# A squared-ReLU MLP whose first product takes both parts of the tokens as one 512-column operand

## The chip, the core and the metric

The kernel runs on one NeuronCore of one Trainium2 chip. Its time is the device time of one execution in microseconds (us). The profile is of one more such execution, taken by the hardware profiler, and it gives the span from the first to the last instruction. The engines are named as in the profile: PE is the matrix engine and PEld its weight loads, ACT is ScalarE, DVE is VectorE, POOL is GpSimd, SP issues most of the DMAs.

## The reference

A two-layer decoder trunk on 256 tokens of 1024 features in float32. Layer 0 is stick-breaking attention and an MLP; a K/V projection is shared by three attention branches; layer 1 is the three-branch sparse attention and an MLP; a last RMSNorm ends it. Both MLPs are the part that is changed:

```python
def sqrelu_mlp(x, w1, w2):
    h = jax.nn.relu(x @ w1)
    return (h * h) @ w2

h = h + sqrelu_mlp(rms_norm(h, norm_gain[layer, 1]), mlp_w1[layer], mlp_w2[layer])
```

with w1 of 1024 x 4096 and w2 of 4096 x 1024, for each of two layers.

## The kernel before

Every large product is made from operands that are split in two parts, a high one (rounded to the matrix engine's float32 form) and a low one (the rest). A product of two split operands is three matmuls: high by high, high by low, low by high. The helper `mm3` (L124 to L127) issues these three for one stationary and one moving operand, each with a weight load of its own.

All 256 tokens are held transposed, features on the 128 partitions: `xt_tiles` (L194) allocates a tile for the high parts (`xh`) and one for the low parts (`xl`), each of 8 feature blocks by 256 tokens, 8 KB a partition. `xt_tr` (L174) transposes four feature blocks of the residual stream on PE into two banks, and `xt_evac` (L184) brings them out: ACT writes the high part with the gain (L190), DVE the low part (L191).

The weights come as one stream of pieces of 1 MB in the order of use. `fetch` issues a piece's DMA on SP; `split` (L79) makes half a piece into its high part on ACT (L89) and its low part on DVE (L90); `step` calls it ahead of need, at most two pieces ahead of the one in use, and three buffers each hold raw, high and low pieces.

An MLP (L227) works in 16 chunks of 256 hidden units. `first(c)` (L250) multiplies: for each of 8 feature blocks k and each of two 128-wide halves f, one `mm3` with a block of w1 as the stationary operand and the 256 tokens as the moving one, so 48 matmuls of 256 columns and 48 loads in a chunk. Both halves of the result lie side by side in one bank (`pu`). Then ACT takes the ReLU of the bank (`mr`, L262), DVE multiplies the bank with it (`ms`, L264), ACT writes the high part (`hh`, L268) and DVE the low one (`hl`, L269). `second` (L234) multiplies the result of an earlier chunk with w2: 24 matmuls of 512 columns into four banks (`acc`) that are summed over all chunks. Chunk c's result is used after `first(c + 1)`; the last two chunks are multiplied together at the end of the MLP. In the first chunk the second half of the feature blocks is still to be transposed: `xt_tr(1)` and `xt_evac` stand between the feature blocks 1 and 2, and no `second` follows before `first(1)`.

The banks `pu` come from a pool of four (`bank2`) that the transposes use too. The 8 KB tiles (`big`) come from a pool of six buffers. The order of instructions on each engine is laid out ahead by the framework's planner, from the program's order and its estimated durations: in the trace some instructions stand ahead of others that come earlier in the text.

Of the kernel before, what the change touches and what calls it, by code (L numbers as in the profile page):

```python
# [7 lines left out]
F32 = mybir.dt.float32  # L8
# [3 lines left out]
OP = mybir.AluOpType  # L12
# [24 lines left out]
def hybrid_kernel(ctx, tc, x, eye, gcols, gfin, wqk, wv, wo0, wkv, wqa, wqb, wqc, wo1, w1, w2, cw1, cw2, cpos, gate_b, consts, out):  # L37
# [10 lines left out]
        return a.bitcast(F32)  # L48

    def big(shape, dt, name):  # L50
        return cp.tile(shape, dt, tag="e", name=name, bufs=6)

    def bank(name, dt=F32):
        return ps.tile([P, 512], dt, tag="a", name=name, bufs=4)
# [1 line left out]
    def bank2(name):  # L56
        return ps.tile([P, 512], F32, tag="z", name=name, bufs=4)

    # the weights in the order of their use: loaded ahead, split in two exact parts
    stream = []  # L60

    def feed(src, n):
# [14 lines left out]
                nc.sync.dma_start(raws[-1], src)  # L77

    def split():  # L79
        """the next half of a piece, split"""  # L80
        j, half = divmod(parts[0], 2)
        parts[0] += 1
        n = stream[j][1]
        if half == 0:
            made.append((wp.tile([P, n], F32R, tag="wh", name="wh", bufs=3),
                         wp.tile([P, n], F32R, tag="wl", name="wl", bufs=3)))
        r = slice(half * n // 2, (half + 1) * n // 2)
        h, lo = made[j]
        nc.scalar.copy(h[:, r], raws[j][:, r])  # L89
        nc.vector.tensor_sub(lo[:, r], raws[j][:, r], f32(h[:, r]))  # L90
        if half:
            fetch()
# [36 lines left out]
    def mm(o, a, b, first, last):  # L129
        nc.tensor.matmul(o, a, b, start=first, stop=last, skip_group_check=True)  # L130

    def tok(xt, k, t):
        return xt[0][:, k, t * P:(t + 1) * P], xt[1][:, k, t * P:(t + 1) * P]

# [19 lines left out]
    npow = cst[:, C_PW:C_PW + 1]  # L154

    def var_of(parts_):
        """mean of squares plus eps, per token"""
        ss = sp.tile([P, 2], F32, name="ss")
        for i, src in enumerate(parts_):
            sq = sp.tile([P, D], F32, name="sq", tag="y")  # L160
            tc.keep_in_program_order(
                nc.scalar.activation(sq[:, 0:src.shape[1]], src, AF.Square, accum_out=ss[:, i:i + 1]))
        v = sp.tile([P, 1], F32, name="v", bufs=4)
        if len(parts_) == 2:
            nc.vector.tensor_add(ss[:, 0:1], ss[:, 0:1], ss[:, 1:2])
        nc.vector.tensor_scalar(v, ss[:, 0:1], 1.0 / D, EPS, op0=OP.mult, op1=OP.add)
        return v
# [4 lines left out]
        return r  # L172

    def xt_tr(half):  # L174
        """four feature blocks of the residual stream, transposed; even blocks in one bank, odd ones in the other"""
        pt = [bank2(f"pt{b}").rearrange("p (j q) -> p j q", j=2) for b in range(2)]
        for b in range(2):
            for j in range(2):
                k = 4 * half + 2 * j + b
                for t in range(T):  # L180
                    nc.tensor.transpose(pt[b][:, j, t * P:(t + 1) * P], hres[t][:, k * P:(k + 1) * P], ident)
        return pt

    def xt_evac(pt, half, gi, xt):  # L184
        """times the gain of each feature, split in two"""
        for j in range(2):
            for b in range(2):
                k = 4 * half + 2 * j + b
                g = gc[:, gi * NK + k:gi * NK + k + 1]
                nc.scalar.activation(xt[0][:, k, :], pt[b][:, j, :], AF.Copy, scale=g)  # L190
                nc.vector.scalar_tensor_tensor(xt[1][:, k, :], pt[b][:, j, :], g, f32(xt[0][:, k, :]),  # L191
                                               op0=OP.mult, op1=OP.subtract)

    def xt_tiles(tag):  # L194
        return big([P, NK, T * P], F32R, f"xh{tag}"), big([P, NK, T * P], F32R, f"xl{tag}")

    def o_evac(oT, po, p):
        nc.scalar.copy(oT[0][:, p, :], po[:, 0:T * P])
# [26 lines left out]
                        res(n, t, acc[n][t])  # L225

    def mlp(layer, gi, xt, mid, ap):  # L227
        """xt holds the first half of the blocks already; mid runs inside the last products"""
        wa, wb = i_m[layer]
        acc = [[None, None], [None, None]]  # L230
        held = []
        r2 = []

        def second(items, order, hook=None):  # L234
            for i, (t, n) in enumerate(order):
                if hook is None and i % 2 == 0:
                    step()
                for c, hT, w in items:
                    for f in range(2):
                        if c == 0 and f == 0:  # L240
                            acc[n][t] = bank(f"acc{t}{n}")
                        mm3(acc[n][t], tok(hT, f, t), cut(w, f * D + n * 512, f * D + (n + 1) * 512),
                            c == 0 and f == 0, c == NFC - 1 and f == 1)
                if hook is not None:
                    hook(i, t, n)

        by_n = [(t, n) for n in range(2) for t in range(T)]
        by_t = [(t, n) for t in range(T) for n in range(2)]

        def first(c):  # L250
            w = W(wa[c])
            pu = bank2("pu")
            for k in range(NK):
                if c == 0 and k == 2:
                    xt_evac(xt_tr(1), 1, gi, xt)
                if k % 4 == 0 and (c or k):
                    step()
                for f in range(2):
                    mm3(pu[:, f * 256:(f + 1) * 256], cut(w, k * 256 + f * P, k * 256 + (f + 1) * P),
                        both(xt, k), f == 0 and k == 0, k == NK - 1)  # L260
            r = ap.tile([P, 512], F32, name="mr")
            nc.scalar.activation(r, pu, AF.Relu)  # L262
            s = ap.tile([P, 512], F32, name="ms")
            nc.vector.tensor_mul(s, pu, r)  # L264
            hh = ap.tile([P, 2, T * P], F32R, name="hh", bufs=3)
            hl = ap.tile([P, 2, T * P], F32R, name="hl", bufs=3)
            sv = s.rearrange("p (f q) -> p f q", f=2)
            nc.scalar.copy(hh, sv)  # L268
            nc.vector.tensor_sub(hl, sv, f32(hh))  # L269
            return hh, hl  # L270

        for c in range(NFC):
            hT = first(c)
            if c == 0:
                for t in range(T):
                    r = sp.tile([P, 1], F32, name="r2", bufs=4)
                    nc.vector.reciprocal(r, var_of([hres[t]]))
                    r2.append(r)
            if 0 < c < NFC - 1:
                second([held.pop(0) + (W(wb[c - 1]),)], by_n)  # L280
            held.append((c, hT))

        def hook(i, t, n):
            res(n, t, acc[n][t], r2[t])
            mid(i)

        second([it + (W(wb[it[0]]),) for it in held], by_t if layer else by_n, hook)

    def layer0(ap):
# [1 line left out]
        warm = bank2("warm")  # L291
        for i in range(8):
            mm(warm, zero[:, 0:P], zero, True, True)
# [44 lines left out]
            for n in range(2):  # L338
                nc.scalar.activation(v[:, t, n * 512:(n + 1) * 512], pv[t][n], AF.Copy, scale=rstd[t])

        oT = big([P, NP, T * P], F32R, "oT_h"), big([P, NP, T * P], F32R, "oT_l")

        live = {}

# [74 lines left out]
        return xn  # L419

    def nsa(xk, pt0, ap):
# [1 line left out]
        gbs = ap.tile([P, 48], F32, name="gbs")  # L423
        nc.scalar.dma_start(gbs, gate_b.to_broadcast([P, 48]))
        pos = ap.tile([P, 2, 16], F32, name="pos")
# [7 lines left out]
                nc.scalar.activation(dst, src, AF.Copy, scale=rstd[t])  # L433

        kd0 = big([P, T, 2 * NG, 2, DH], F32, "kd0")
        kd = [[ap.tile([P, NG, 2, DH], F32, name=f"kd{br}{t}") for t in range(T)] for br in range(2)]
        vs = [ap.tile([P, 2, 256], F32, name=f"vs{t}") for t in range(T)]
        pts = [pt0]
        rstd = []
# [27 lines left out]
        sin = cst[:, C_SIN:C_SIN + 32].rearrange("p (t r) -> p t r", t=T)  # L467

        def rope(src, t, n):
            """src[:, h, 0:16] rotated in place; sin holds (-sin, sin), cos (cos, cos)."""  # L470
            a = ap.tile([P, n, 16], F32, name="ropea", tag=f"ropea{n}")
            b = ap.tile([P, n, 16], F32, name="ropeb", tag=f"ropeb{n}")
            c = cos[:, t:t + 1, :].to_broadcast([P, n, 16])
# [4 lines left out]
            nc.gpsimd.tensor_mul(b[:, :, 8:16], src[:, :, 0:8], s1)  # L478
            nc.gpsimd.tensor_add(src[:, :, 0:16], a, b)

        # compressed blocks: windows of the transposed keys and values, plus positions
        M = NG * NC
        blk = [None, None]

# [26 lines left out]
            nc.vector.tensor_sub(bs[:, :, 1, 0:M], bt, f32(bs[:, :, 0, 0:M]))  # L511
            blk[c] = bs

        # keys of the selected and window branches: rotated, transposed, on either half of the partitions, split
        def keys_rope(br):
            for t in range(T):
                rope(kd[br][t].rearrange("p g a d -> p (g a) d"), t, 2 * NG)
# [31 lines left out]
        gather(1)  # L549
        keys_rope(1)  # L550

        # compressed keys and values
        kT = [big([P, NG, 2, T * P], F32R, f"kT{i}") for i in range(2)]
        ph = bank("ph")
        cw_proj(0, 0)
        keys_tr(0)
# [14 lines left out]
        nc.scalar.activation(hu, hu, AF.Exp, scale=-1.0)  # L571
        nc.vector.tensor_mul(hu, hu, hx)

# [1 line left out]
        gates = ap.tile([P, T, 48], F32, name="gates")  # L575

        def q_proj(n, mid=None):
# [86 lines left out]
                nc.vector.tensor_tensor(vcb[:, g], pvc[0:M, g * DH:(g + 1) * DH][:, None, :].to_broadcast([M, 4, DH]),  # L664
                                        cst[0:M, C_BLK:C_BLK + 4][:, :, None].to_broadcast([M, 4, DH]), op=OP.mult)

        # compressed branch: probabilities times gates, transposed, for heads 8 * hf .. 8 * hf + 7
        def cmp_probs(hf):
            for t in range(T):
                pc = bank("psc")  # L670
# [30 lines left out]
        nc.gpsimd.tensor_copy(w2d, cw2s[:, 0, :, None, :].to_broadcast([P, 2, 2, DH]))  # L701
        vcb = ap.tile([M, NG, 4, DH], F32, name="vcb")
        pcT = ap.tile([M, NG, T * P], F32, name="pcT")
        # selected and window branches, and the gated sum of all three
        cb = cam_b[:, None, :].to_broadcast([P, 2, P])

        def scores(h):
# [92 lines left out]
        turn(0)  # L800
        cmp_tr(0)
        q_rot(r[2], 10, 6)
        oT = big([P, NP, T * P], F32R, "oT_h"), big([P, NP, T * P], F32R, "oT_l")
        scores(3)
        scale(2)
        turn(1)
# [82 lines left out]
def _layout(inp):  # L889
# [4 lines left out]
        return np.ascontiguousarray(v)  # L894

    def blocks(w, nk, cw):
        """[K, N] -> [N / cw, K / (nk * 128), 128, nk * cw]"""
        k, n = w.shape
        return cont(w.reshape(k // (nk * P), nk, P, n // cw, cw).transpose(3, 0, 2, 1, 4)
                    .reshape(n // cw, k // (nk * P), P, nk * cw))  # L900
# [46 lines left out]
```

## Time and profile before

| | |
|---|---|
| time, median of 3 runs | 657.2 us (655.12 to 657.46) |
| span of the profiled execution | 654.1 us |
| PE busy | 640.1 us (98%), 4096 matmuls |
| PEld busy | 563.6 us (86%), 4096 loads |
| DVE busy | 397.3 us (61%) |
| ACT busy | 352.2 us (54%) |
| POOL busy | 57.9 us (9%) |
| DMA | 106.87 MB, mean 163 GB/s |

The profile has no time of the profiled execution other than its span; the three runs lie 1.0 to 3.3 us above that span, which is what lies around the first and the last instruction and the spread from run to run. A busy PE is one with a matmul in its pipe: matmuls overlap, so busy time does not add up to the time that they take from the engine. That is read from the starts of successive matmuls instead.

### The profile page before, as it was taken

To read this page: it belongs to the slowest core of one execution; us is meant where nothing else is said; L and a number is where in the kernel's file an instruction comes from. 1 tells how busy PE (TensorE), PEld (TensorE's weight loads), DVE (VectorE), ACT (ScalarE), POOL (GpSimd) and SP (SyncE) were. 2 spreads that over 40 slices of the span, in tenths; PEclk is the share of its full clock that TensorE was granted. 3 is DMA by queue.
4 is the path that set the end of the run, shared out by engine and by line. 5 is a ranking of instruction groups with operands and counts; after the bars stand their busy time and mean duration, and the time that the engine had idled before them with its cause. 6 is when DMAs were issued, how large, how long until landed. Compare 5 with 4: busy or idle time off the path is not lost.

```text
span 654.1 us, 10023 instructions
## 1 busy us (share of the span) xinstructions
PE 640.1 (98%) x4096; PEld 563.6 (86%) x4096; DVE 397.3 (61%) x558; ACT 352.2 (54%) x588; POOL 57.9 (9%) x91
## 2 busy tenths in 40 slices
PE   8999999999999999999999999999999999999995
PEld 5899887899999998988888987767998989999994
DVE  5665554675454545555899888773765555454544
ACT  5776676364444444444866767662464454444433
POOL 1000000000000000000133334550000000000000
PEclk9999999999999999999999999999999999999999
DMA  8853332545555554555545750101555555555501
GB/s 325 299 181 126 128 97 98 174 147 193 194 193 194 178 196 164 198 171 187 202 156 177 264 191 2 66 1 63 178 195 180 194 189 193 192 193 193 178 18 64
DMA packets 16894, 106.87 MB, mean 163 GB/s; under 512 B 2256, under 2 KB 2512, under 8 KB 4944
## 3 DMA queue, kind: packets, MB, share of 16 engines
q1 hardware_dynamic: 15696, 104.92, 45.5%
q10 hardware_dynamic: 1152, 1.31, 0.7%
q8 instruction: 32, 0.52, 0.3%
q14 instruction: 14, 0.11, 0.0%
HBM read 105.17 MB, written 1.05 MB: 162 GB/s over the span
## 4 chain that ended last, share of the span: by engine, by line
PE 87%; ACT 4%; DVE 4%; DMA 2%; POOL 2%; issue 1%; SPq 0%; POOLq 0%; ACTq 0%; DVEq 0%
PE acc L125 11%; PE acc L126 11%; PE acc L127 11%; PE pu L126 9%; PE pu L127 9%; PE pu L125 9%; PE po L130 4%; PE qk L125 2%; PE qk L126 2%; ACT wh L89 2%; PE qk L127 2%; PE z L130 2%; PE pk L127 2%; PE pk L126 2%; PE pk L125 2%
## 5 line engine op out<-in xcount | busy, mean ns | idle before, releaser
L90 DVE TENSOR_TENSOR wl<-raw,wh 128x1024 fp32r<-128x1024 f32 (+3 forms) x202 | 237.6, 1200 | 181.5 <-ACT wh L89 181.1
L89 ACT CAST wh<-raw 128x1024 fp32r<-128x1024 f32 (+3 forms) x202 | 200.3, 1023 | 213.1 <-issue 103.8
L126 PE MATMUL pu<-xln,wh 128*128 128x256 f32 x512 | 145.0, 283 | 0.0
L127 PE MATMUL pu<-xhn,wl 128*128 128x256 f32 x512 | 144.9, 283 | 0.0
L125 PE MATMUL pu<-xhn,wh 128*128 128x256 f32 x512 | 144.5, 283 | 0.0
L125 PE MATMUL acc<-wh,hh 128*128 128x512 f32 x256 | 100.0, 392 | 0.0
L126 PE MATMUL acc<-wl,hh 128*128 128x512 f32 x256 | 99.7, 391 | 0.0
L126 PEld LDWEIGHTS pu<-xln,wh 128*128 128x128 f32 x512 | 98.1, 192 | 1.4 <-DVE xln L191 0.2
L127 PE MATMUL acc<-wh,hl 128*128 128x512 f32 x256 | 99.2, 389 | 0.0
L125 PEld LDWEIGHTS pu<-xhn,wh 128*128 128x128 f32 x512 | 98.0, 192 | 1.2
L127 PEld LDWEIGHTS pu<-xhn,wl 128*128 128x128 f32 x512 | 98.1, 192 | 0.0
L127 PEld LDWEIGHTS acc<-wh,hl 128*128 128x128 f32 x256 | 48.1, 188 | 10.5 <-DVE hl L269 0.2
L125 PEld LDWEIGHTS acc<-wh,hh 128*128 128x128 f32 x256 | 48.2, 188 | 9.6 <-ACT hh L268 0.5
L126 PEld LDWEIGHTS acc<-wl,hh 128*128 128x128 f32 x256 | 48.2, 188 | 8.8
L125 PE MATMUL qk<-xha,wh 128*128 128x256 f32 x128 | 36.8, 288 | 0.0
L127 PE MATMUL qk<-xha,wl 128*128 128x256 f32 x128 | 36.3, 283 | 0.0
L126 PE MATMUL qk<-xla,wh 128*128 128x256 f32 x128 | 36.2, 283 | 0.0
L739 POOL TENSOR_TENSOR pe<-pe,rs 128x256 f32<-128x256 f32 (+1 forms) x32 | 26.2, 841 | 25.5 <-DVE rs L735 19.8
L268 ACT CAST hh<-ms 128x512 fp32r<-128x512 f32 x32 | 19.9, 622 | 14.6 <-DVE ms L264 14.6
L699 POOL MEMSET kcb<- 128x120 f32 x1 | 0.2, 200 | 291.1 <-PE acc L127 291.1
L125 PE MATMUL acc<-wh,oT_h 128*128 128x512 f32 x64 | 25.6, 400 | 0.0
L125 PEld LDWEIGHTS qk<-xha,wh 128*128 128x128 f32 x128 | 24.5, 191 | 1.1 <-issue 1.0
(188 smaller groups left out, 972.3 us busy)
## 6 DMA issues: line engine op xcount, KB each, us to landing
raw<-in_w SPq DMA_DIRECT2D x64, 1024.0 KB, 4.8
raw<-in_wqk SPq DMA_DIRECT2D x8, 1024.0 KB, 4.9
raw<-in_wo SPq DMA_DIRECT2D x8, 1024.0 KB, 4.8
raw<-in_wkv SPq DMA_DIRECT2D x6, 1024.0 KB, 5.0
raw<-in_cw SPq DMA_DIRECT2D x4, 1024.0 KB, 5.1
raw<-in_wv SPq DMA_DIRECT2D x3, 1024.0 KB, 7.1
raw<-in_wqb SPq DMA_DIRECT2D x2, 768.0 KB, 4.2
raw<-in_wqc SPq DMA_DIRECT2D x2, 768.0 KB, 5.2
```

The lines of the kernel that those rows point to most:

```text
L89: nc.scalar.copy(h[:, r], raws[j][:, r])
L90: nc.vector.tensor_sub(lo[:, r], raws[j][:, r], f32(h[:, r]))
L125: nc.tensor.matmul(o, a[0], b[0], start=first, stop=False, skip_group_check=True)
L126: nc.tensor.matmul(o, a[0], b[1], start=False, stop=False, skip_group_check=True)
L127: nc.tensor.matmul(o, a[1], b[0], start=False, stop=last, skip_group_check=True)
L130: nc.tensor.matmul(o, a, b, start=first, stop=last, skip_group_check=True)
L268: nc.scalar.copy(hh, sv)
L699: nc.gpsimd.memset(kcb, 0.0)
L739: nc.gpsimd.tensor_tensor(s, s, rs[:, t, :][:, :, None].to_broadcast([P, 2, n]), op=OP.mult)
```

## The change

In the first product the high and the low part of the tokens become one moving operand of 512 columns. One wide matmul with the high weights makes both products at once: high by high in columns 0 to 255 of a bank, high by low in columns 256 to 511. A second matmul with the low weights and the high tokens adds its 256 columns to the first half of the bank. Each half f of the chunk now fills a bank of its own, and (but in the first four feature blocks of the first chunk) the banks are filled one after the other. So a chunk has 16 matmuls of 512 and 16 of 256 columns, and 32 loads. The two halves of a bank are then added: ACT copies the upper half to SBUF, DVE adds it to the lower one, and DVE makes max(u, 0) times u in one instruction for the chunk. `hh` and `hl` are made as before.

For the wide operand to be contiguous, the two parts of the tokens lie interleaved by feature block in one tile of 16 KB. There are two such tiles (`x`), which the split attention outputs (`oT`) and keys (`kT`) use too; the pool of 8 KB tiles has three buffers instead of six, and takes the keys `kd` as one tile.

```diff
     def big(shape, dt, name):
-        return cp.tile(shape, dt, tag="e", name=name, bufs=6)
+        return cp.tile(shape, dt, tag="e", name=name, bufs=3)
+
+    def pair(shape, name):
+        return cp.tile([P, 2, *shape], F32R, tag="x", name=name, bufs=2)
...
+    def wide(o, a, xt, k, first, last):
+        mm(o, a[0], xt[2][:, k, :, :], first, False)
+        mm(o[:, 0:T * P], a[1], xt[0][:, k, :], False, last)
...
     def xt_tiles(tag):
-        return big([P, NK, T * P], F32R, f"xh{tag}"), big([P, NK, T * P], F32R, f"xl{tag}")
+        xp = cp.tile([P, NK, 2, T * P], F32R, tag="x", name=f"x{tag}", bufs=2)
+        return xp[:, :, 0, :], xp[:, :, 1, :], xp
...
         def first(c):
             w = W(wa[c])
-            pu = bank2("pu")
-            for k in range(NK):
-                if c == 0 and k == 2:
+            pu = [bank2(f"pu{f}") for f in range(2)]
+            r = ap.tile([P, 512], F32, name="mr")
+            u = ap.tile([P, 512], F32, name="mu")
+            s = ap.tile([P, 512], F32, name="ms")
+
+            ks = [(f, k) for k in range(NK // 2) for f in range(2)] + [(f, k) for f in range(2) for k in range(NK // 2, NK)]
+            for i, (f, k) in enumerate(ks if c == 0 else [(f, k) for f in range(2) for k in range(NK)]):
+                if c == 0 and i == 4:
                     xt_evac(xt_tr(1), 1, gi, xt)
-                if k % 4 == 0 and (c or k):
+                if i % 8 == 0 and (c or i):
                     step()
-                for f in range(2):
-                    mm3(pu[:, f * 256:(f + 1) * 256], cut(w, k * 256 + f * P, k * 256 + (f + 1) * P),
-                        both(xt, k), f == 0 and k == 0, k == NK - 1)
-            r = ap.tile([P, 512], F32, name="mr")
-            nc.scalar.activation(r, pu, AF.Relu)
-            s = ap.tile([P, 512], F32, name="ms")
-            nc.vector.tensor_mul(s, pu, r)
+                wide(pu[f], cut(w, k * 256 + f * P, k * 256 + (f + 1) * P), xt, k, k == 0, k == NK - 1)
+                if k == NK - 1:
+                    q = slice(f * 256, (f + 1) * 256)
+                    nc.scalar.copy(r[:, q], pu[f][:, 256:512])
+                    nc.vector.tensor_add(u[:, q], pu[f][:, 0:256], r[:, q])
+            nc.vector.scalar_tensor_tensor(s, u, 0.0, u, op0=OP.max, op1=OP.mult)
...
-        oT = big([P, NP, T * P], F32R, "oT_h"), big([P, NP, T * P], F32R, "oT_l")
+        oT = pair([NP, T * P], "oT")
+        oT = oT[:, 0], oT[:, 1]
...
-        kd = [[ap.tile([P, NG, 2, DH], F32, name=f"kd{br}{t}") for t in range(T)] for br in range(2)]
+        kdt = big([P, 2, T, NG * 2 * DH], F32, "kd")
+        kd = [[kdt[:, br, t, :].rearrange("p (g a d) -> p g a d", g=NG, a=2) for t in range(T)] for br in range(2)]
...
-        kT = [big([P, NG, 2, T * P], F32R, f"kT{i}") for i in range(2)]
+        kT = pair([NG, 2, T * P], "kT")
+        kT = kT[:, 0], kT[:, 1]
```

## Rows read from the trace of the kernel before

**Rows 1.** The page's first part: busy time, share, number of instructions.

```profile
PE 640.1 (98%) x4096; PEld 563.6 (86%) x4096; DVE 397.3 (61%) x558; ACT 352.2 (54%) x588; POOL 57.9 (9%) x91
```

**Rows 2.** The chain that ended last, by engine.

```profile
PE 87%; ACT 4%; DVE 4%; DMA 2%; POOL 2%; issue 1%; SPq 0%; POOLq 0%; ACTq 0%; DVEq 0%
```

**Rows 3.** Windows, one chunk of layer 0: length, busy times, granted clock, DMA share, GB/s.

```profile
181.90:193.12 11.22, 11.22 (x74) 10.26 (x72) 5.92 (x6) 5.10 (x6) 0.00 (x0) 1.00 0.54 188
```

**Rows 4.** Timeline of PE through that chunk: start us, length us, instruction.

```profile
181.90 0.28 PE L125 MATMUL pu<-xhn,wh 128*128 128x256 f32 x1
182.01 0.28 PE L126 MATMUL pu<-xln,wh 128*128 128x256 f32 x1
...
187.65 0.40 PE L125 MATMUL acc<-wh,hh 128*128 128x512 f32 x1
187.88 0.40 PE L126 MATMUL acc<-wl,hh 128*128 128x512 f32 x1
...
189.04 0.39 PE L125 MATMUL acc<-wh,hh 128*128 128x512 f32 x1
...
192.89 0.39 PE L127 MATMUL acc<-wh,hl 128*128 128x512 f32 x1
193.12 0.28 PE L125 MATMUL pu<-xhn,wh 128*128 128x256 f32 x1
```

**Rows 5.** Timeline of PE, first and last of 16 matmuls of 384 columns.

```profile
371.14 0.33 PE L127 MATMUL pq<-wh,xlq 128*128 128x384 f32 x1
...
373.74 0.34 PE L127 MATMUL pq<-wh,xlq 128*128 128x384 f32 x1
```

**Rows 6.** Groups by line and shape, the weight loads: busy us, mean ns, idle before.

```profile
L126 PEld LDWEIGHTS pu<-xln,wh 128*128 128x128 f32 x512 | 98.1, 192 | 1.4 <-DVE xln L191 0.2
```

**Rows 7.** Groups by line and shape, ACT and DVE.

```profile
L198 ACT CAST oT_h<-po 128x256 fp32r<-128x256 f32 x16 | 6.0, 375 | 9.8 <-PE po L130 9.8
L199 DVE TENSOR_TENSOR oT_l<-po,oT_h 128x256 fp32r<-128x256 f32 x16 | 6.7, 421 | 11.7 <-ACT oT_h L198 11.7
L206 DVE SCALAR_TENSOR_TENSOR hres<-acc,r,hres 128x512 f32<-128x512 f32 x8 | 6.0, 748 | 4.6 <-PE acc L127 4.6
```

**Rows 8.** Timeline of DVE and ACT in that chunk.

```profile
183.22 2.36 DVE L90 TENSOR_TENSOR wl<-raw,wh 128x1024 fp32r<-128x1024 f32 x2 [2.03 <-ACT wh L89]
...
191.73 0.68 DVE L269 TENSOR_TENSOR hl<-ms,hh 128x512 fp32r<-128x512 f32 x1
```

**Rows 9.** Timeline of the first chunk of layer 0, then of layer 1.

```profile
132.36 0.36 PE L125 MATMUL pu<-xhn,wh 128*128 128x256 f32 x1
...
133.74 0.87 DVE L191 SCALAR_TENSOR_TENSOR xln<-pt,gc,xhn 128x256 fp32r<-128x256 f32 x2
...
134.27 0.39 PE L126 MATMUL pu<-xln,wh 128*128 128x256 f32 x1
...
134.76 0.88 DVE L191 SCALAR_TENSOR_TENSOR xln<-pt,gc,xhn 128x256 fp32r<-128x256 f32 x2
...
469.57 0.36 PE L127 MATMUL pu<-xhn,wl 128*128 128x256 f32 x1
...
470.03 0.88 DVE L191 SCALAR_TENSOR_TENSOR xln<-pt,gc,xhn 128x256 fp32r<-128x256 f32 x2 [0.73 <-ACT xhn L190]
470.83 1.22 DVE L90 TENSOR_TENSOR wl<-raw,wh 128x1024 fp32r<-128x1024 f32 x1
471.96 0.87 DVE L191 SCALAR_TENSOR_TENSOR xln<-pt,gc,xhn 128x256 fp32r<-128x256 f32 x2
```

**Rows 10.** Timeline of the last chunk of layer 1.

```profile
636.47 0.60 ACT L262 ACTIVATE mr<-pu 128x512 f32<-128x512 f32 x1 [3.71 <-PE pu L127]
...
637.10 0.69 DVE L264 TENSOR_TENSOR ms<-pu,mr 128x512 f32<-128x512 f32 x1 [2.90 <-ACT mr L262]
...
637.83 0.62 ACT L268 CAST hh<-ms 128x512 fp32r<-128x512 f32 x1 [0.76 <-DVE ms L264]
...
638.34 0.66 PE L125 MATMUL acc<-wh,hh 128*128 128x512 f32 x2
```

More of the change, by code (lines that the diff above doesn't have):

```diff
@@ L802, in nsa @@
         q_rot(r[2], 10, 6)
-        oT = big([P, NP, T * P], F32R, "oT_h"), big([P, NP, T * P], F32R, "oT_l")
+        oT = pair([NP, T * P], "oT")
+        oT = oT[:, 0], oT[:, 1]
         scores(3)
```

## The prediction

> **What bounds the kernel now.** First the busy table: PE has 98% of the span, DVE 61%, ACT 54% [rows 1]. As PE's busy time hides gaps between overlapping matmuls, the chain of waits is next: 87% of it is PE itself, no other engine has over 4% [rows 2]. So the span is mostly the sum of what matmuls take from PE one after the other. For the stretch that is changed I read a window over one chunk: 11.22 us, PE and PE alone busy all through, the granted clock at 1.00 (the 2.4 GHz level), DVE busy 5.92 and ACT 5.10 us, DMA at 0.54 [rows 3]. There are 32 such chunks, some 359 of 654 us. What a matmul really costs is the distance between starts in PE's timeline, not its 0.28 or 0.40 us of length. From 181.90 to 187.65 there are 48 matmuls of 256 columns: 5.75 us, 0.120 each. From 187.65 to 193.12 there are 24 of 512 columns: 5.47 us; the last 17 steps of them, 189.04 to 192.89, are 0.2265 each [rows 4]. And 15 steps of 384 columns, 371.14 to 373.74, are 0.173 each [rows 5]. The three lie on one line: 128 more columns cost 0.053 us, and a matmul of no columns would still cost 0.013 us. So each matmul (with its weight load) has a fixed part of 13 ns, 11% of a 256-column one. That fixed part is what the change can save: the number of columns stays the same, 12,288 a chunk.
>
> **The matmuls.** A chunk loses 48 matmuls of 256 columns and gets 16 of 512 and 16 of 256. One pair costs 0.2265 + 0.120 = 0.3465 us, 16 pairs 5.54 instead of 5.75: 0.21 a chunk, over 32 chunks -6.6 us. All of it lies on the path, as PE is the chain.
>
> No row shows 512 and 256 alternating. At the change from 512 to 256 the first short step is 0.11, and at the change back the first long one 0.23 [rows 4]: together 0.34, so a pair of neighbours costs about its sum, which is the value I take. From the other side: after a change the long ones need some steps to settle, 187.65 to 189.04 being six in 1.39 us, 0.232 each. If the pairs never settle they cost 0.352, a chunk 5.63, and the gain is 0.12 x 32 = 3.8 us. If on the other hand the second product no longer needs to settle, 6 x 0.005 = 0.03 a chunk comes on top, -7.5 us. The sum 0.3465 is nearest to the measured change-over.
>
> The Trainium skill, "TensorE: Matmul & The Clock Gate", section "Back-to-back issue gap", speaks against this gain: it gives the gap at full clock as the columns at 2.4 GHz and about 2.5 ns on top. By that, 512 matmuls fewer would be an estimated 1.3 us, a fifth. The rows at 256, 384 and 512 columns have 13 ns instead, and the sum goes by them.
>
> **The evacuation, in the steady chunks.** Before: one ReLU of 512 columns on ACT, one product on DVE. After: two copies of 256 columns on ACT and two sums on DVE; their nearest rows, of the same shape out of a bank, are 0.375 and 0.421 [rows 7]. Then one combined instruction of 512 columns on DVE, between 0.685 (the low part's subtraction, 0.68 in rows 8) and 0.748 [rows 7]. ACT gets 2 x 0.375 for 0.60: +0.15 a chunk; DVE gets 0.84 + 0.7 for 0.69: +0.85. DVE is then busy 6.8 of 11.0 us, ACT 5.3. I cost this at nothing. Its cover: the low part of a chunk is ready at 192.41 (191.73 + 0.68), while the matmuls that read it follow the next chunk's first product, about 198.9 (193.12 + 5.75): 6.4 us to spare. The split weights that wait behind on the same queues are done at 185.58 [rows 8] and used from 193.12: 7.5 us. An added 1 us uses up neither. If the cover were gone, each microsecond of lateness would cost 32 us.
>
> The banks: a chunk now takes two of the four, filled in turn, the first one free for reading 8 pairs (2.8 us) before the chunk ends. A bank is wanted again two chunks later, after 11 us, but in the first chunk: there the transposes hold two, and the next chunk follows at once. They are given back by the last low part of the tokens, before the first chunk's end; I cost it at nothing, and at a wait of one copy and one sum (0.8) in each layer as its upper end.
>
> **The first chunk of each layer.** A wide matmul reads the low tokens too, so it waits for DVE where the high by high product needed ACT alone; and the last four feature blocks are now used up by the first half f alone, at 0.35 a block instead of 0.72. Layer 0: PE goes on at 132.36 and has four pairs before block 4, so it is there about 133.83. The low parts of blocks 4 and 5 take 133.74 to 134.61, of 6 and 7 134.76 to 135.64 [rows 9]. Block 4 waits 0.35, 5 0.1, 6 0.25, 7 0.1: 0.8, of which PE already waits some 0.25 now (the matmul at 134.27 is 0.15 behind the count, the next 0.1): +0.5. Layer 1: PE goes on at 469.57 with two pairs and a third to do, so it is at block 4 about 470.46. Blocks 4 and 5 are ready at 470.47 and 470.91; then a half weight of 1.22 stands before blocks 6 and 7, which come at 472.40 and 472.83 [rows 9]. In strict order PE would wait about 1.2; if the planner puts the other half's blocks 4 and 5 ahead, 0.5. Now it waits 0.15. I take +0.5 for this layer too: +1.0 in all, with ends at 0.2 (the planner fills every wait) and 1.6.
>
> **The last chunk of each layer.** There the evacuation has only the 24 matmuls of the chunk before for cover. Now ReLU, product and high part take 636.47 to 638.45, and the first matmul that needs them comes behind 638.34 with about 0.1 of wait [rows 10]. After: copy 0.375, sum 0.421, combined 0.72, high part 0.62: 2.14 instead of 1.91, and one hand-over more: +0.3. The first bank's copy and sum are done earlier and don't count. PE waits at these points already, so it is late by most of that: +0.2 a layer, +0.4; ends -0.2 and 1.0.
>
> **The storage.** The 16 KB tiles and the three 8 KB buffers are each taken again only after PE work that comes earlier in PE's own order: the outputs' pair follows the last query projection, the keys' pair the last K/V projection, the second compressed block the transposes that it is computed from. The keys' slices in one tile are disjoint. No DMA is moved or added, and SP's queue waits for the same splits. Nothing new is late: 0, with one DVE instruction (0.5) to either side.
>
> **The sum.** -6.6 + 1.0 + 0.4 = -5.2 on a span of 654.1: 648.9. The runs' median is 3.1 above the span; that part, launch and spread, is unchanged. 657.2 - 5.2 = 652.0.
>
> **Rivals.**
>
> *The pairs don't settle, and the edges cost their upper ends.* -3.8 + 1.6 + 1.0 = -1.2: 656.0, no change that can be told. For it: every row of 512 columns right after a change is 5 to 9 ns over the settled ones. Against it: the step after is shorter by as much (0.11 for 0.12). Chance 0.13.
>
> *The change doesn't do what it says:* the fixed part goes with each 256 columns, the wide operand being run as two pieces. Then the matmuls cost what they cost now and the edges' 1.4 is lost: 658.6, no change. Against it stand three widths on one line [rows 4, 5], the widest with one fixed part. Chance 0.07. By the page named above ("TensorE: Matmul & The Clock Gate" of the Trainium skill, the same section) the estimate is 657.2 - 1.3 + 1.4 = 657.3, close to this case.
>
> *More than counted.* The second product settles at once and the planner fills the first and last chunks: -7.5 + 0.2 - 0.2 = -7.5: 649.7. For it: the planner already orders PE's matmuls around these waits. Chance 0.14.
>
> *The other side: a load that the short matmul does not cover.* Each load takes 192 ns [rows 6], and the short matmul ahead of a wide one occupies PE for 120. If loads did not overlap each other, the wide matmul would wait 72 ns more: 512 x 0.072 = 37 us against a gain of 6.6: about 689, slower. It decides from 10 ns a pair on (5.2 / 512), and from 17 ns ((5.2 + 3.3) / 512) the kernel is slower by more than 3.3 us. Against it: in the stream of 256 columns every load has just such a matmul ahead of it, and the steps are still 0.120. So two loads overlap now. Chance 0.05.
>
> **How the numbers follow.** 0.5% of the time is 3.3 us, about what a measurement of this kernel can tell from no change: faster is below 653.9, slower above 660.5. My forecast, 652.0, has 0.61. Its own unknowns reach from -7.5 to about -3, so nearly all of it is faster (0.58), the rest the same. With the case of a larger gain faster has 0.72; the unsettled pairs and the split operand give the same with 0.03 + 0.13 + 0.07 = 0.23; slower 0.05. The range reaches from 649.4 (the larger gain, and a median that falls lower in its spread) to 656.0 (the unsettled pairs with the edges' upper ends). It leaves out the other two cases and the tails.
>
> **What would show it.** Right: in PE's timeline of a steady chunk, steps of 0.227 and 0.120 in turn, a first product of 5.55 us and a chunk of 11.0. No PE wait for `hh`, `hl` or split weights between the second and the last chunk. In the first chunks PE waits of half a microsecond on the low tokens (L191), in the last ones of a few tenths on the high part. Wrong: a pair at 0.352 or more, which takes 3 us of the gain; at 0.36, which takes all; or a PE wait that comes back in every chunk.

## The result, and the profile after

The changed kernel takes 652.0 us (median of 4 runs, 651.2 to 652.6), the kernel before 657.1 in the same comparison (655.1 to 657.5). The ratio is 0.9933, with a 95% interval from 0.9915 to 0.9952: 4.4 us less, between 3.1 and 5.6 (the two medians themselves lie 5.1 apart). Its profiled execution has a span of 650.8 us and a time of 652.6; 1.8 us lie around the span.

The page after, with the busy table and the chain by engine, for [rows 1] and [rows 2]:

```profile
PE 636.9 (98%) x3584; PEld 536.9 (82%) x3584; DVE 420.4 (65%) x622; ACT 356.7 (55%) x620; POOL 57.0 (9%) x91
...
PE 84%; DVE 6%; ACT 4%; POOL 2%; issue 2%; DMA 1%; POOLq 0%; SPq 0%; ACTq 0%; DVEq 0%
```

There are 512 matmuls and loads fewer, and PE is still the chain. To see where the time went, the span is cut at the starts of the stages. Windows of the kernel before: the start, layer 0's attention, its MLP, K/V and queries, layer 1's attention, its MLP, the tail. The columns are length, busy time of PE, PEld, DVE, ACT and POOL, granted clock, DMA share, GB/s.

```profile
0.00:31.31 31.31, 29.28 (x124) 21.99 (x125) 19.21 (x27) 20.39 (x30) 4.58 (x10) 1.00 0.85 307
31.31:130.13 98.82, 98.12 (x697) 85.77 (x696) 56.53 (x71) 61.51 (x94) 0.00 (x0) 1.00 0.39 136
130.13:311.90 181.77, 181.77 (x1169) 165.86 (x1168) 99.71 (x112) 86.16 (x108) 0.00 (x0) 1.00 0.52 183
311.90:386.59 74.69, 73.16 (x440) 66.16 (x439) 65.34 (x97) 49.99 (x78) 22.50 (x39) 1.00 0.58 203
386.59:466.75 80.16, 77.13 (x510) 59.06 (x510) 55.46 (x138) 48.50 (x171) 29.71 (x40) 1.00 0.18 59
466.75:647.05 180.30, 180.30 (x1160) 164.75 (x1159) 98.91 (x113) 84.21 (x107) 0.55 (x1) 1.00 0.47 167
647.05:654.13 7.08, 0.39 (x2) 0.00 (x0) 2.09 (x4) 1.45 (x3) 0.55 (x1) 0.85 0.21 80
```

The same stages of the changed kernel:

```profile
0.00:32.31 32.31, 29.56 (x125) 22.57 (x125) 18.70 (x27) 20.24 (x30) 2.88 (x10) 0.95 0.80 302
32.31:131.16 98.85, 98.15 (x697) 85.79 (x696) 56.51 (x71) 61.51 (x94) 0.00 (x0) 1.00 0.37 136
131.16:311.25 180.09, 179.79 (x913) 151.88 (x912) 110.86 (x141) 87.52 (x122) 0.00 (x0) 1.00 0.50 184
311.25:385.83 74.58, 73.15 (x440) 66.11 (x439) 66.14 (x99) 50.65 (x81) 22.52 (x39) 1.00 0.55 203
385.83:464.83 79.00, 77.26 (x511) 59.64 (x510) 55.64 (x139) 48.63 (x171) 30.52 (x40) 0.98 0.18 68
464.83:643.75 178.92, 178.62 (x904) 150.87 (x903) 110.48 (x144) 86.68 (x123) 0.55 (x1) 1.00 0.45 164
643.75:650.80 7.05, 0.39 (x2) 0.00 (x0) 2.09 (x4) 1.45 (x3) 0.55 (x1) 0.90 0.21 81
```

Read line against line: +1.00 in the start, where the granted clock is lower (0.95 against 1.00), nothing in layer 0's attention, -1.68 and -1.38 in the two MLPs, -1.16 in layer 1's attention, -0.14 in the rest: -3.3 on these two spans. Without the start, which belongs to the execution (below), it is -4.3. So the MLPs gave 3.06 us and not the 5.2 that was forecast for them, and 1.2 came from a stage where nothing was forecast.

A steady chunk, for [rows 3], is 11.11 us instead of 11.22, not 11.0:

```profile
182.58:193.69 11.11, 11.11 (x58) 9.41 (x56) 6.68 (x9) 5.26 (x7) 0.00 (x0) 1.00 0.57 187
```

PE's timeline at its beginning, for [rows 4], shows why (start us, length us, instruction):

```profile
182.58 0.39 PE L134 MATMUL pu<-xn,wh 128*128 128x512 f32 x1
182.81 0.28 PE L134 MATMUL pu<-xn,wl 128*128 128x256 f32 x1
182.92 0.40 PE L134 MATMUL pu<-xn,wh 128*128 128x512 f32 x1
183.16 0.28 PE L134 MATMUL pu<-xn,wl 128*128 128x256 f32 x1
183.27 0.40 PE L134 MATMUL pu<-xn,wh 128*128 128x512 f32 x1
...
183.98 0.40 PE L134 MATMUL pu<-xn,wh 128*128 128x512 f32 x1
```

The first wide step is 0.23 and the first narrow one 0.11, as at the change-over in [rows 4]. From 182.92 on three pairs take 1.06 us, 0.353 each, and that goes on to the chunk's end: wide steps of 0.23 to 0.24 and narrow ones of 0.11 to 0.12, with no wide step of 0.227 again. Sixteen pairs take 5.64 us instead of 5.75 for the 48 matmuls.

The first chunk, for [rows 9], of layer 0 (DVE's low parts, and the wide matmul that waits for them):

```profile
134.72 0.28 PE L134 MATMUL pu<-xn,wl 128*128 128x256 f32 x1
...
134.77 0.87 DVE L201 SCALAR_TENSOR_TENSOR xn<-pt,gc,xn 128x256 fp32r<-128x256 f32 x2
...
135.30 0.50 PE L134 MATMUL pu<-xn,wh 128*128 128x512 f32 x1 [0.30 <-DVE xn L201]
135.64 0.27 PE L134 MATMUL pu<-xn,wl 128*128 128x256 f32 x1
```

The wide matmul of feature block 4 starts 0.58 after the one before it, where a narrow step is 0.12: 0.46 of wait; after it (135.64 - 135.30 = 0.34) 0.11 more. The last chunk of layer 1, for [rows 10]:

```profile
632.96 0.40 PE L129 MATMUL acc<-wh,hh 128*128 128x512 f32 x1
633.16 0.37 ACT L278 COPY mr<-pu 128x256 f32<-128x256 f32 x1 [2.46 <-PE pu L134]
...
633.56 0.42 DVE L279 TENSOR_TENSOR mu<-pu,mr 128x256 f32<-128x256 f32 x1 [2.23 <-ACT mr L278]
634.02 0.69 DVE L280 SCALAR_TENSOR_TENSOR ms<-mu 128x512 f32<-128x512 f32 x1
...
634.75 0.62 ACT L284 CAST hh<-ms 128x512 fp32r<-128x512 f32 x1 [1.22 <-DVE ms L280]
...
635.47 0.44 PE L129 MATMUL acc<-wh,hh 128*128 128x512 f32 x1
```

From the copy's start to the end of the high part it is 2.21 us, against 1.98 in [rows 10]. But PE is not later by that. In the kernel before the products with w2 that end the MLP begin here:

```profile
636.27 0.40 PE L125 MATMUL acc<-wh,hh 128*128 128x512 f32 x1
```

From there to the last of them, which opens the tail, it is 10.78 us (to 647.05); in the changed kernel 10.79 (632.96 to 643.75).

### The profile page after: what moved, and what is told of

It reads as the page before. It is cut to its first block, busy times and chain, and to the rows that moved or that the text cites. A ratio compares the mean times of both kernels' runs of the same rounds, so it can differ in the third digit from the quotient of the medians.

```text
span 650.8 us, 9102 instructions
## 1 busy us (share of the span) xinstructions
PE 636.9 (98%) x3584; PEld 536.9 (82%) x3584; DVE 420.4 (65%) x622; ACT 356.7 (55%) x620; POOL 57.0 (9%) x91
## 4 chain that ended last, share of the span: by engine, by line
PE 84%; DVE 6%; ACT 4%; POOL 2%; issue 2%; DMA 1%; POOLq 0%; SPq 0%; ACTq 0%; DVEq 0%
PE pu L134 27%; PE acc L129 11%; PE acc L130 11%; PE acc L131 11%; PE po L134 3%; ACT wh L93 2%; PE qk L129 2%; PE qk L130 2%; DVE wl L94 2%; PE qk L131 2%; PE pk L131 2%; PE pk L130 2%; PE pk L129 2%; PE z L134 1%; PE pv L129 1%
## 5 line engine op out<-in xcount | busy, mean ns | idle before, releaser
L134 PE MATMUL pu<-xn,wh 128*128 128x512 f32 x512 | 181.9, 398 | 0.6 <-DVE xn L201 0.6
L134 PE MATMUL pu<-xn,wl 128*128 128x256 f32 x512 | 142.9, 280 | 0.0
L134 PEld LDWEIGHTS pu<-xn,wh 128*128 128x128 f32 x512 | 95.9, 188 | 24.1 <-DVE xn L201 1.2
L134 PEld LDWEIGHTS pu<-xn,wl 128*128 128x128 f32 x512 | 96.6, 189 | 1.5
L278 ACT COPY mr<-pu 128x256 f32<-128x256 f32 x64 | 23.6, 369 | 28.2 <-PE pu L134 28.2
L129 PE MATMUL qk<-xa,wh 128*128 128x256 f32 x128 | 36.8, 288 | 0.0
L131 PE MATMUL qk<-xa,wl 128*128 128x256 f32 x128 | 36.3, 283 | 0.0
L130 PE MATMUL qk<-xa,wh 128*128 128x256 f32 x128 | 36.2, 283 | 0.0
L285 DVE TENSOR_TENSOR hl<-ms,hh 128x512 fp32r<-128x512 f32 x32 | 22.1, 691 | 20.0 <-ACT hh L284 20.0
L279 DVE TENSOR_TENSOR mu<-pu,mr 128x256 f32<-128x256 f32 x64 | 26.7, 417 | 5.0 <-ACT mr L278 5.0
L129 PE MATMUL acc<-wh,oT 128*128 128x512 f32 x64 | 25.6, 400 | 0.0
```

The source lines that it names most:

```text
L129: nc.tensor.matmul(o, a[0], b[0], start=first, stop=False, skip_group_check=True)
L130: nc.tensor.matmul(o, a[0], b[1], start=False, stop=False, skip_group_check=True)
L131: nc.tensor.matmul(o, a[1], b[0], start=False, stop=last, skip_group_check=True)
L278: nc.scalar.copy(r[:, q], pu[f][:, 256:512])
L279: nc.vector.tensor_add(u[:, q], pu[f][:, 0:256], r[:, q])
```

## The experiments

Two theories of the pair's price were open after the profile: the change of width costs PE something each time it goes back to 512 columns, or these wide matmuls are slow by themselves (their operand, their bank). And the 1.2 us in layer 1's attention could be the storage, or chance.

**Storage alone.** The changed storage with the first product as it was:

```diff
-            pu = [bank2(f"pu{f}") for f in range(2)]
...
+            pu = bank2("pu")
+            for k in range(NK):
...
+                    mm3(pu[:, f * 256:(f + 1) * 256], cut(w, k * 256 + f * P, k * 256 + (f + 1) * P),
+                        both(xt, k), f == 0 and k == 0, k == NK - 1)
```

> The first product as before (three matmuls of 256 columns, one bank a chunk), on the changed storage: tokens' parts interleaved in tiles of 16 KB, three buffers of 8 KB. Theory A (all of the gain is the matmuls, the storage does nothing): 657.1, ratio to before 1.000 within 0.002; attention of layer 1 between its last query projection and its MLP 80.2 us as before. Rival B (part of the gain is the storage, through another order of layer 1's attention, where the changed kernel's profile is 1.2 us shorter): 655.9, ratio 0.998, that stretch 79.0 us.

Measured: 655.0 us against 655.7, ratio 0.9988 (0.9979 to 0.9998). Its chunks are 11.22 us, its MLPs 181.80 and 180.53, and layer 1's attention is

```profile
386.85:465.81 78.96, 75.97 (x510) 58.40 (x510) 55.68 (x139) 48.63 (x171) 30.54 (x40) 1.00 0.20 67
```

80.16 before. The whole run's ratio alone would fit either theory, and its interval nearly reaches 1; the stage decides. This 1.2 us is the storage's doing: rival B holds. The stage's idle time on PE is the same (80.16 - 77.13 = 3.03 us before, 78.96 - 75.97 = 2.99 here); it is PE's busy time that is 1.16 shorter, for the same 510 matmuls in another order. At one place of PE's timeline the kernel before has two score matmuls apart, with transposes between them:

```profile
406.01 0.48 PE L130 MATMUL z<-kT,qs 128*128 128x512 f32 x1
406.32 0.38 PE L748 MATMUL ptp<-ident,pe 128*128 128x128 f32 x2
406.46 0.48 PE L130 MATMUL z<-kT,qs 128*128 128x512 f32 x1
```

and with the changed storage they come together, the transposes after them:

```profile
406.27 0.71 PE L134 MATMUL z<-kT,qs 128*128 128x512 f32 x2
...
407.06 0.27 PE L762 MATMUL ptp<-ident,pe 128*128 128x128 f32 x1
```

This place shows that the order is another, not where the time is gained. That the planner orders by the points where tiles come free is argued, not shown, and which of the storage edits moves it was not separated.

The storage also takes something back. In the kernel before, the first chunks of layer 1's MLP, from its start to the first product with w2, take 12.44 us, in layer 0 12.64; on the changed storage both take 12.64.

**The kernel before once more.**

> The kernel before once more, for a second profile of it. If the stages of one kernel repeat to 0.1 us from execution to execution, the attention of layer 1 takes 80.2 us again and only the first 8 us, where the input's DMAs land, differ. Ratio 1.000. If the stage moves by 1 us by itself, the 1.2 us that the changed kernel gained there are no effect of the change.

Measured: ratio 0.9995 (0.9984 to 1.0006); span 655.7, 1.6 longer than the first one. Layer 1's attention is 80.17, the MLPs 181.77 and 180.30:

```profile
388.17:468.34 80.17, 77.13 (x511) 59.05 (x510) 55.46 (x138) 48.49 (x171) 29.71 (x40) 1.00 0.17 60
```

Behind the start the stages repeat to 0.04 us. The start differs, 32.85 against 31.31, and not in the first 8 us, as expected, so much as from 8.5 us on, where PE's granted clock is lower. Windows of PE over the first stretch with feature transposes and value products: this execution, the first one of before, and the changed kernel, each with length, PE busy, clock, DMA share, GB/s.

```profile
8.50:12.00 3.50, 3.46 (x13) 0.52 1.02 422
```

```profile
8.50:12.00 3.50, 3.50 (x20) 1.00 1.02 423
```

```profile
8.50:12.00 3.50, 3.50 (x15) 0.63 1.00 411
```

With the clock at half (the 1.2 GHz level) for all or most of this stretch 13 to 15 matmuls get through where 20 do at full clock. Over all ten profiled executions, layer 0's MLP begins at 131.1 to 131.7 us in the three with such a stretch in the start, one of them of the unchanged kernel, and at 129.6 to 130.6 in the other seven. So the start's +1.0 is no effect of the change.

**Wide ones first, narrow ones after, by half and by chunk.** The first chunk of each layer is left as it was. By chunk:

```diff
-                wide(pu[f], cut(w, k * 256 + f * P, k * 256 + (f + 1) * P), xt, k, k == 0, k == NK - 1)
...
+                for f in range(2):
+                    step()
+                    for k in range(NK):
+                        hi(f, k)
+                for f in range(2):
+                    for k in range(NK):
+                        low(f, k)
```

where `hi` is the matmul of 512 columns of a pair and `low` that of 256, with the copy and the sum after the last one. By half, both loops over k stand in one loop over f.

> The changed kernel with each half's eight wide matmuls first and its eight narrow ones after them (in the first chunk of each layer as it was). Theory A (each return from 256 to 512 columns costs PE some 7 ns; the changed kernel has 16 a chunk, this one 2): a chunk 11.03 us instead of 11.107, 30 chunks: 2.4 us less than the changed kernel, 649.6, ratio to before 0.989. Rival B (the wide matmul in this bank is slow by itself, 0.235, whatever stands before it): chunk 11.107, 652.0, ratio 0.993.

> The same with all sixteen wide matmuls of a chunk first and the sixteen narrow ones after them: one return to 512 columns a chunk, at the second product. Theory A: a chunk 11.01 us, 30 chunks: 3.0 us less than the changed kernel, 649.0, ratio to before 0.988. Rival B: chunk 11.107, 652.0, ratio 0.993. Rival C (the first bank is ready only 1 us before the second, so the evacuation comes late): PE waits for the high part in each chunk, slower than the run with halves.

Measured: by half 649.2 us, ratio 0.9901 (0.9887 to 0.9914); by chunk 648.9, ratio 0.9897 (0.9884 to 0.9911). Steady chunks are 11.027 and 11.007 by their starts, where theory A had 11.03 and 11.01. PE's timeline by half: eight wide ones in 1.81 us after wide ones, eight in 1.84 after narrow ones.

```profile
180.87 1.98 PE L134 MATMUL pu<-xn,wh 128*128 128x512 f32 x8
182.68 1.11 PE L134 MATMUL pu<-xn,wl 128*128 128x256 f32 x8
183.63 2.00 PE L134 MATMUL pu<-xn,wh 128*128 128x512 f32 x8
185.47 1.11 PE L134 MATMUL pu<-xn,wl 128*128 128x256 f32 x8
```

By chunk, sixteen wide ones take 3.63 us, 0.227 each, and sixteen narrow ones 1.91, 0.119 each:

```profile
182.28 3.79 PE L134 MATMUL pu<-xn,wh 128*128 128x512 f32 x16
185.91 2.08 PE L134 MATMUL pu<-xn,wl 128*128 128x256 f32 x16
187.82 0.40 PE L129 MATMUL acc<-wh,hh 128*128 128x512 f32 x1
```

The same matmuls of the same operands into the same banks run at the settled price once the order is changed. Rival B falls, and rival C too: no steady chunk waits. The MLPs by chunk:

```profile
131.09:309.93 178.84, 178.53 (x914) 152.28 (x912) 111.29 (x143) 86.66 (x123) 0.00 (x0) 1.00 0.53 186
463.64:641.25 177.61, 177.30 (x905) 151.26 (x903) 110.48 (x144) 85.35 (x123) 0.55 (x1) 1.00 0.47 167
```

That is 2.6 us less than in the changed kernel, of the 3.0 expected, and 5.6 less than before. Layer 1's attention takes 78.96 by chunk, as with the storage alone. By half it takes 80.04, with a granted clock of 0.96 over the stage: one of the short stretches of lower clock fell into it in that execution.

**No change of width at all.** The second matmul of each pair takes the whole 512 columns; it then adds the product of the low parts too.

```diff
-        mm(o[:, 0:T * P], a[1], xt[0][:, k, :], False, last)
+        mm(o, a[1], xt[2][:, k, :, :], False, last)
```

> The changed kernel with the second matmul of each pair widened to 512 columns too (it adds the product of the two low parts to the upper half), so that the stationary operands alternate as before but no step changes width. Theory A (the excess of 6.7 ns a pair comes from the change of width): 32 steps of 0.2267 in a steady chunk, first product 7.25 us, kernel 652 + 32 x 1.61 = 703.6. Rival (it comes from the alternation of high and low weights, or from this bank or tile): the steps stay at 0.230 to 0.241 on every other matmul, first product 7.36 us or more.

Measured: 701.2 us (one run). The steps:

```profile
201.37 0.39 PE L134 MATMUL pu<-xn,wh 128*128 128x512 f32 x1
201.60 0.39 PE L134 MATMUL pu<-xn,wl 128*128 128x512 f32 x1
...
202.96 0.39 PE L134 MATMUL pu<-xn,wl 128*128 128x512 f32 x1
```

Seven steps in 1.59 us, 0.227 each, with high and low weights alternating as in the changed kernel. So it is the change of width; what in PE costs it, no run shows. The kernel is 2.4 us below the 703.6 expected, 0.8 of it because the second product, with no narrow matmul ahead of it, no longer has to settle (5.44 us by its starts instead of 5.47); the rest was not taken apart.

**The two parts of the operand apart.**

```diff
-        xp = cp.tile([P, NK, 2, T * P], F32R, tag="x", name=f"x{tag}", bufs=2)
-        return xp[:, :, 0, :], xp[:, :, 1, :], xp
+        xp = cp.tile([P, 2, NK, T * P], F32R, tag="x", name=f"x{tag}", bufs=2)
+        return xp[:, 0], xp[:, 1], xp
...
-        mm(o, a[0], xt[2][:, k, :, :], first, False)
+        mm(o, a[0], xt[2][:, :, k, :], first, False)
```

> The changed kernel with its two 256-column parts of the wide operand 8 KB apart in the tile instead of side by side. Theory A (a matmul has one fixed part, whatever its operand's pattern): steps as in the changed kernel, 227 to 241 and 113 to 120 ns, first product 5.64 us, ratio to before 0.993. Rival (the operand is run as two pieces of 256 and pays the fixed part twice, which the contiguous layout avoids): wide steps of 0.240 to 0.254, 13 ns more for 16 a chunk, 0.21 us a chunk, 6.7 us, ratio 1.003.

Measured: 651.8 us, ratio 0.9931 (0.9910 to 0.9953), as the changed kernel; a steady chunk:

```profile
182.12:193.22 11.10, 11.10 (x57) 9.41 (x56) 6.67 (x9) 5.26 (x7) 0.00 (x0) 1.00 0.54 190
```

A moving operand in two pieces is one matmul with one fixed part. The interleaved layout was not needed for the gain.

**The evacuation twice.**

```diff
-                    nc.scalar.copy(r[:, q], pu[f][:, 256:512])
-                    nc.vector.tensor_add(u[:, q], pu[f][:, 0:256], r[:, q])
+                    for _ in range(2):
+                        nc.scalar.copy(r[:, q], pu[f][:, 256:512])
+                        nc.vector.tensor_add(u[:, q], pu[f][:, 0:256], r[:, q])
```

> The changed kernel with each copy and each sum of the evacuation made twice. Theory A (in the steady chunks the evacuation has 6 us of cover and costs nothing): chunk 11.107 us unchanged, PE waits longer only in the last chunk of each layer, by at most 0.8 us a layer: 652.0 to 653.6. Rival (ACT or DVE is near enough to its limit that the added 1.6 us a chunk delays split weights or the high part): chunk over 11.2 us, over 655.

Measured: 653.0 us, ratio 0.9949 (0.9930 to 0.9969). A steady chunk:

```profile
181.73:192.83 11.10, 11.10 (x57) 9.40 (x56) 7.53 (x10) 6.01 (x10) 0.00 (x0) 1.00 0.56 193
```

DVE and ACT are each 0.8 us busier in it and PE loses nothing; the MLPs are 0.42 and 0.44 us longer as a whole (180.51 and 179.36). Of that 0.27 and 0.26 lie in the first two chunks, which the expectation left out, and 0.14 and 0.18 behind the last first product. The cover is real in the steady chunks, and not full at the edges.

**The first chunk grouped too.**

```diff
+                for k in range(NK):
+                    if k == 2:
+                        xt_evac(xt_tr(1), 1, gi, xt)
+                    if k == 4:
+                        for f in range(2):
+                            for kk in range(4):
+                                low(f, kk)
+                        step()
+                    for f in range(2):
+                        hi(f, k)
+                for f in range(2):
+                    for k in range(4, NK):
+                        low(f, k)
```

> The run with sixteen wide matmuls and then sixteen narrow ones in a chunk, with the first chunk grouped too: the narrow matmuls of the first four feature blocks stand before the wide ones of the last four, which then come in pairs by feature block. Theory A (the first chunk of a layer loses some 0.6 us to waits for the last low parts, and the alternation there costs as elsewhere): 0.5 us less a layer, 1.0 less than 648.9: 647.9, ratio to before 0.988. Rival (the waits only move): 648.9, ratio 0.9897.

Measured: 649.5 us, ratio 0.9898 (0.9879 to 0.9917). The MLPs take 178.92 and 177.71, against 178.84 and 177.61 when grouped by chunk alone: the rival holds, the waits only move. In the first chunk DVE's low parts of the last blocks (from 133.21) stand behind 2.36 us of split weights, and the wide matmul that needs them starts at 133.75, some 0.5 us after PE could have gone on:

```profile
130.93 2.36 DVE L94 TENSOR_TENSOR wl<-raw,wh 128x1024 fp32r<-128x1024 f32 x2 [0.44 <-ACT wh L93]
...
133.75 2.44 PE L134 MATMUL pu<-xn,wh 128*128 128x512 f32 x9 [0.32 <-DVE xn L201]
```

## Why the prediction was right

The time was forecast at 652.0 and came out at 652.0, with the sign, and within its range. But three of its terms were off, and the base was too. By its own sign, "a pair at 0.352 or more, which takes 3 us of the gain", its main term failed.

- **The matmuls (-6.6 forecast, -3.6 measured).** This is the term that was mis-sized. The step that failed: "together 0.34, so a pair of neighbours costs about its sum, which is the value I take". The change-over in [rows 4] shows the first pair only. Each further pair costs 0.353, what the unsettled steps of the same group had given (0.352): 16 x 0.353 = 5.64, 0.112 a chunk, 32 x 0.112 = 3.6. The rival of pairs that don't settle had the price about right (a gain of 3.8); its 656.0 did not come because the edges cost less than it charged and the storage gave something. Grouped by chunk, a steady chunk gains what was forecast for it: 11.220 - 11.007 = 0.213, which over 32 chunks would be 6.8 (30 were grouped).
- **The fixed part.** It goes with the matmul, as read off three widths: 0.227 and 0.119 in the grouped kernel, and one fixed part even for an operand in two pieces. The rival by which the change would not do what it says falls. The 2.5 ns of the Trainium skill ("TensorE: Matmul & The Clock Gate", section "Back-to-back issue gap"), by which 657.3 was estimated, are given there for a single matmul by itself, and the section says that in a stream of loads and matmuls both set the spacing; the prediction left that out. These float32 matmuls have a load each, and their settled steps have a fixed part of about 13 ns, with 7 more for each pair of alternating widths.
- **The load under the short matmul.** No wide step is over 0.24 in a steady chunk, so nothing of 72 ns is exposed. That rival falls.
- **The evacuation at nothing.** Right for the steady chunks: doubled, it still costs them nothing.
- **The edges (+1.4 forecast, +0.5 measured).** The MLPs gained 3.06 where the pairs gave 3.58. The first chunk of layer 0 waits 0.57 for the low parts, 0.25 before. The first chunks cost 0.6, where 1.0 was forecast, and 0.2 of that is the storage's (layer 1's 12.44 became 12.64 with the old product, and is 12.59 with the new one). At the end of an MLP the evacuation is 0.2 longer, as worked out, but PE loses nothing (10.79 us against 10.78 in layer 1, 11.97 against 12.05 in layer 0). The forecast charged that length as if it were a wait.
- **The storage (0 forecast, -1.2 measured in layer 1's attention).** No wait was added there, as argued, but the order of PE's matmuls changed, and that order is shorter. The step that failed is to cost an edit of storage by its waits alone; its bounds (0.5) were too narrow. Alone it took 0.8 us off the run (0.1 to 1.4).
- **The second product.** It settles no faster than before (5.47 us in a steady chunk), so the case of a larger gain did not come either.
- **The base.** The forecast subtracted its 5.2 from the median of three runs, 657.2. In the two later comparisons the kernel before has 655.7 (21 runs) and 656.2 (7 runs). Of the 3.1 us between the first profile's span and 657.2, 1.8 lie around the span. For the rest a slower start is likely: a second profile of the kernel before, at 657.5 us, has the half clock in its start, the first one has not. It is not shown, since no clock is on record for those runs. Where one is, it goes with the time: 26 later runs of the kernel before at a mean granted clock of 0.997 or more have a median of 655.6, 13 at a lower one 656.7. Of the changed kernel's four runs, two at 0.997 took 651.2 and 651.4, two at 0.994 both 652.6. At the higher clock the two kernels, though measured in different comparisons, lie 4.3 apart, as their stages do without the start.

So an overestimate of 3.0 in the matmuls was made good by 0.9 of edges that were not paid, 1.2 from the storage, and the rest, about 0.9, almost all by a base that was high. The sign and the place of the gain were reasoned; that the time came out to the tenth is luck.

The version grouped by chunk has the lowest median of all that were run: 648.9 us, ratio 0.9897 to the kernel before, against 0.9933 for the changed one.

## What to carry to other kernels

Where PE is the chain, price matmuls by the distance of their starts at several widths: what is left at no columns is saved with each matmul that is merged into a wider one. Keep matmuls of one width together; alternating widths gave back about half of the matmuls' gain here, and a new order of the loops got most of it back (2.6 of 3.0 us). And read a stage's length against a second execution of the same kernel before a microsecond is put down to an edit: here the stages behind the start repeat to 0.04 us, but the start does not, nor does a stage into which a stretch of half clock falls, and storage alone can change the order of a stage far away.

## What the runs showed of the hardware that was not expected

- A matmul of 512 columns after one of 256 costs more than the settled 0.227: with widths alternating, a pair is 0.353 instead of 0.347; coming back once from sixteen narrow ones to 24 wide ones costs the second product 0.03 us (5.47 against 5.44 with no narrow ones).
- PE's granted clock fell to half for a few microseconds in some executions. In the start it did so with the DMA queues full (a mean of 0.52 and 0.63 from 8.5 to 12 us, where these executions' starts are 1.0 to 1.5 us longer); ahead of it, from 4 to 8.5 us, PE was busy 2.69 us in the second execution of the kernel before and 3.66 in the first, whose clock did not fall. In layer 1's attention it did so with hardly any DMA: 1.1 us of the stage in the version grouped by half (80.04 against 78.96), next to nothing in the changed kernel (79.00). What triggers it was not tried.
